# Hybrid decoder layer on one core: dilated tiles in groups of two, the narrow pattern's mask by a product and its sums on two engines, guards in groups of six

## The chip, the core and the metric

The kernel runs on one core of a Trainium2 chip. The metric is the device time of one execution in microseconds, as a median of several runs. Engines are named as in the profile: PE (TensorE, products), PEld (its weight loads), DVE (VectorE), ACT (ScalarE), POOL (GpSimd), SP (SyncE, which here issues nearly all transfers). The granted clock of PE is given as a share of its full rate.

## What is computed

One decoder layer over 2048 positions of width 1024. Eight heads of a dilated attention (three patterns of window and stride, with a linear bias per head, merged by their softmax denominators) and eight heads of a causal latent attention, each gated by SiLU, go through one output projection and a layer norm with the residual:

```python
DILATED_PATTERNS = ((128, 1), (512, 4), (2048, 16))

def _dilated_mixture(q, k, v):
    slopes = _alibi_slopes(q.shape[2])
    parts = [_dilated_pattern(q, k, v, slopes, w, d) for (w, d) in DILATED_PATTERNS]
    m_all = jnp.max(jnp.stack([pm for (_, pm, _) in parts], axis=0), axis=0)
    num = 0.0
    den = 0.0
    for acc, pm, pl in parts:
        wgt = jnp.exp(pm - m_all)
        num = num + acc * wgt[..., None]
        den = den + pl * wgt
    return num / den[..., None]
```

`_dilated_pattern` scores each query against the keys of its residue class in the window (`q.k / 8` minus slope times distance, masked by causality and window) and returns numerator, row maximum and denominator. All is float32.

## The kernel before

The program has five stages in a row, all unrolled: projections with keys and latent vectors (to 441 us), the gates with the guards (441 to 679), the dilated attention (679 to about 935), the latent attention (to about 1345), and the output projection with the layer norm.

*Order.* Every PE instruction goes through `Order` (`pe`), which pins them one behind the other as written. `pe.plan(work, span)` holds a list of side jobs, and `pe.tick()` after each main product lets one go whenever its share of `span` has passed. In the attention stages ACT is pinned the same way (`act`), and SP (`sp`). `later(units, f)` puts a job off by so many tiles; `go_on(w)`, called behind each tile's scores, counts them down and runs what is due. Loads of the next pair (`LT`), the rotated copies of its keys (`LTO`), and the steps of the division all go through it.

*Gates and guards.* 32 main tiles of 24 products (`m_tile`, a bank `mm` of six) make the SiLU gates. Between them run the guards: for each pair of heads 96 small rough score tiles in bfloat16 (32 for each pattern: keys contiguous, every 4th, every 16th), of which only the row maxima are wanted. `block(g)` (L752) does two guards: two products into one bank of the tag `nm` (two banks), then two reductions with the bias on DVE (L758). A pair's 48 blocks are followed by the load for the next pair, three empty items, `last` (transposes and scatters the maxima through DRAM), `GPAUSE` = 5 empty items; `write`, the fetch of the merged maxima, is set into the next pair's blocks at place `GW`. All items are spread over 623 main products.

*Dilated attention.* Four pairs of heads. A pair is a stream of 20 score tiles (`attend`, L962): four units of three tiles for the two wide patterns (two of stride 4, one of stride 16), then four units of two tiles for the narrow one. A tile's scores (`scores`, L967) are, for each of the two heads, a bfloat16 product `X` and an fp32r product `Y` (`KY`, `QY`), added in one PSUM bank of the tag `s` (four banks), and an exponential on ACT into `e` or `more` (seven buffers). Where `late(which)` holds (L965), `strike` (L983) zeroes what the mask forbids with selects on POOL (L990): two for stride 1 and 4, one for stride 16; otherwise a product of `identb` with the mask `msk` goes ahead of the scores. Before, that is so only for the narrow tiles of the last pair. `r_` then multiplies the values (`pv`, `o`). At a unit's end `finish` sums the exponentials into `acc`: on DVE, but in the last pair's narrow units on POOL (L1063 to L1068). One tile behind a narrow unit comes `epilogue(c)` (L1076): gate load, products of `ones` with `acc` (`l`), a copy `ls` on ACT (one buffer), its transfer `u<-ls` from ACT's queue, a reciprocal, and by way of DRAM (`sums`, `r`) the division of `g` and its store to `mixd`.

*Order in the dilated stage.* `chain(stream, g)` (L893) takes `g` tiles' scores, then the values of all held tiles but `LAG`. With `G2` = 1 and `LAG` = 1 the order is s2 r0 s3 r1: values run two tiles behind their scores. From the 13th tile of the last pair on, the guards of the latent attention (`mx<-k,ql`) are planned in between.

Of the kernel before, what the change touches and what calls it, by code (L numbers as in the profile page):

```python
# [9 lines left out]
F32 = mybir.dt.float32  # L10
# [8 lines left out]
P = 128  # L19
# [12 lines left out]
UQE = 20  # L32
SCB = 3
GFIRST = 4
GPAUSE = 5
LEAD = 42
K1T = (1.0, 6, 6.0)
WOT = (16, 18.5, 21, 26, 28, 30)
# [9 lines left out]
NL = 2**LEVELS - 1  # L48
EX = 3 + NL
UADD = 2  # L50
LAG = 1
XSB = 2
WARM = 12
GB = 2
GW = 9
RB = 2
HB = 2
SPL2 = 1
# [4 lines left out]
LTO = {(1, 0): (5, 6, 7, 8), (1, 1): (8.3, 9, 10, 11), (2, 0): (13, 14, 15, 16), (2, 1): (20.2, 21, 22, 23)}  # L63
KT3 = (1.0, 4.0, 14.0, 16.0, 18.0, 17.0, 7.0)
T2 = 0.4
G2 = 1
WSD = 0b0000
WSV = lambda g: WSD >> g & 1
MSV = lambda g: False
EPD = 1  # L70
EPL = 1
WP = 0
WL = 2
OB = 2
EB = 5
# [134 lines left out]
def body(ctx, tc, a, out):  # L210
# [104 lines left out]
    with ExitStack() as p1:  # L315
# [391 lines left out]
        with ExitStack() as p1g:  # L707
# [13 lines left out]
            def guard(p):  # L721
# [28 lines left out]
                            todo.append((n3(q, r), n3(k, r), P, e - 4, m[:, 2, h * 16 + r :]))  # L750

                def block(g):  # L752
                    o = ps.tile([P, 512], F32, tag="nm", name="mx", bufs=2)
                    for i, (q, k, n, e, dst) in enumerate(todo[g : g + 2]):
                        pe.matmul(o[:, i * 256 : i * 256 + n], q, k, start=True, stop=True)
                    for i, (q, k, n, e, dst) in enumerate(todo[g : g + 2]):
                        oi = o[:, i * 256 : i * 256 + n]
                        nc.vector.tensor_tensor_reduce(  # L758
                            out=oi, in0=oi, in1=bias[:, e, 256 - n : 256], scale=1.0,
                            scalar=-3.0e38, op0=ALU.add, op1=ALU.max, accum_out=dst[:, 0:1])  # L760
# [26 lines left out]
                    nc.vector.tensor_tensor(out=nm, in0=u[:, 0, :], in1=u[:, 2, :], op=ALU.min)  # L787
                    dma(nc.sync, out=dqe[2 * p : 2 * p + 2, EX - 1].rearrange("h (s j) -> h s j", j=P), in_=nm)

                return load, [(lambda g=g: block(g)) for g in range(0, 96, 2)], (last, write)  # L790

            extras = []
            for i, (dst, n) in enumerate(((dke, EX), (dqe[:, 0 : EX - 1], EX - 1))):
# [17 lines left out]
            for n, (i, c) in enumerate(seq):  # L811
                if n % 4 == 0 and n < 28:
                    w[n // 4 + 1] = load_w(gates[n // 4 + 1])
                if n == 0:
                    work = [guard(p) for p in range(PAIRS)]
                    work[0][0]()
                    dma(nc.sync, out=perm, in_=a["perm"])
                if n == 12:
                    for dst, src, w_ in ((msk[:, 0:512], a["mst"][:, 0:512], 512), (msk[:, 512:640], a["mst"][:, 512:640], 128),
                                         (mxb[:, 384:512], a["mxm"], 128)):  # L820
                        t = gp.tile([P, CH], F32, tag="v", name="mst", bufs=3)
                        dma(nc.sync, out=t[:, 0:w_], in_=src)
                        nc.gpsimd.tensor_copy(dst, t[:, 0:w_])
                if n == GFIRST:
                    items = []
                    for p, (_, blocks, (last, write)) in enumerate(work):
                        items += blocks + ([work[p + 1][0]] if p + 1 < PAIRS else []) + [pause] * 3 + [last]
                        items += [pause] * GPAUSE
                        if p:
                            items.insert(len(items) - len(blocks) - GPAUSE - 4 + GW, hold)  # L830
                        hold = write
                    items.append(hold)
                    pe.plan(items, (30 - GFIRST) * 24 - 1)
                if XT <= n < XT + len(extras):
                    extra(*extras[n - XT])
                o = m_tile(w[i], c)
                if n == 30:
                    gl = big([P, 2, CH], F32, "gl")
                g = gp.tile([P, CH], F32, tag="v", name="g", bufs=3) if n < 30 else gl[:, n - 30, :]
                (act if n == 31 else nc.scalar).activation(g, o, AF.Silu)  # L840
                dma(nc.sync, out=gat[i * P : (i + 1) * P, c * CH : (c + 1) * CH], in_=g)
                for k in {25: ("k0", "k1", "x0"), 27: ("q0", "x1", "q1"), 29: ("vb", "vc")}.get(n, ()):
                    loads[k]()
                if n >= 28:
                    x, h = ((1, 0), (1, 1), (2, 0), (2, 1))[n - 28]
                    for i in range(4):
                        loads["order"](h, x, i, nc.scalar.copy if i % 2 else nc.gpsimd.tensor_copy)
# [6 lines left out]
    with ExitStack() as p24:  # L854
# [107 lines left out]
        def attend(p, d):  # L962
            acc, osum = [], []

            late = lambda which: p < PAIRS - 1 or which > 0  # L965

            def scores(h, e, which, blocks, first):  # L967
                n = sum(w for _, _, w in blocks)
                s = spsum()
                if not late(which):  # L970
                    pe.matmul(s[:, 0:n], identb, msk[:, 0:n], start=True, stop=False)

                x = 0 if which == 2 and h and first else which
                for y, kq in enumerate("XY"):
                    kt_, qt = (d["X", h][:, 0], d["X", h][:, 1]) if kq == "X" else (d["KY", h, x if y else 0], d["QY", h])
                    off = 0
                    for i, (kf, qf, w) in enumerate(blocks):
                        pe.matmul(s[:, off : off + w], kf[y if x else 0](kt_), qf(qt), start=bool(late(which) and kq == "X" and i == 0),
                                  stop=(kq == "Y" and i == len(blocks) - 1))
                        off += w  # L980
                act.activation(e[:, h, 0:n], s[:, 0:n], AF.Exp, scale=0.125)

            def strike(e, which, n):  # L983

# [11 lines left out]
            def unit(specs, finish, more=None):  # L996
# [3 lines left out]
                def s_(i, w):  # L1000
                    which, blocks = specs[i][:2]
                    e = exps(True)
                    for h in range(2):
                        scores(h, e, which, blocks, first)
                        pe.tick(w * T2)
                    if late(which):
                        strike(e, which, sum(w_ for _, _, w_ in blocks))
                    es.append([e[:, h] for h in range(2)])
# [42 lines left out]
            for c in range(4):  # L1051
# [7 lines left out]
                def finish(o, es, c=c):  # L1059
                    for h in range(2):  # L1060
                        dst = acc[h][:, c * CH : (c + 1) * CH].rearrange("p (r b i) -> p b r i", r=16, b=4)
                        x1, x2 = (e[h].rearrange("p (b r i) -> p b r i", b=4, r=16) for e in es)
                        eng = nc.gpsimd if h < WP or (h < WL and p == PAIRS - 1) else nc.vector  # L1063
                        eng.tensor_add(dst, dst, x1)
                        eng.tensor_add(dst[:, 1:4], dst[:, 1:4], x2[:, 0:3])  # L1065
                        if c:
                            x2 = over[0][h].rearrange("p (b r i) -> p b r i", b=4, r=16)
                            eng.tensor_add(dst[:, 0], dst[:, 0], x2[:, 3])  # L1068
# [6 lines left out]

            def epilogue(c):  # L1076
                cols = slice(c * CH, (c + 1) * CH)
                g = ep.tile([P, 512], F32, tag="g", name="g", bufs=3)
                dma(sp, out=g, in_=gat[p * P : (p + 1) * P, cols])
                nc.vector.tensor_mul(nat(g), strip(osum[c]), nat(g))  # L1080
                divide(acc, cols, g, nat, p * NC + c,
# [94 lines left out]
        def attend3(i):  # L1176
# [13 lines left out]
            gate = []  # L1190

            def load_g():
                gate.append(ep.tile([P, 512], F32, tag="g", name="g3", bufs=3))
                dma(sp, out=gate[0], in_=gat[512 + p * P : 512 + (p + 1) * P, Q * CH : (Q + 1) * CH])

            def s_(two, ws):
# [314 lines left out]
```

## Time and profile before

| | us |
|---|---|
| runs | 1564.69 (median), 1565.36, 1556.76 |
| the profiled execution, as a run | 1558.75 |
| its span on the core | 1557.0 |
| gates and guards, 441 to 661 | 220.0 |
| dilated attention, first three pairs and the last one's wide patterns, 679.2 to 885.6 | 206.4 |

The span is counted from the first to the last instruction. In rows of a timeline `x4` counts instructions run together in the row, the first number is the start and the second the duration in microseconds; products overlap in the array, so the pace is read from one start to the next. In brackets stands how long the engine was idle ahead of the row, and what ended it.

### The profile page before, as it was taken

Reading aid. Unit: us, or ns where it says so; the run is one execution under the profiler, and the core shown is the slowest. Engines: PE = TensorE matmul, PEld = TensorE weight load, DVE = VectorE, ACT = ScalarE, POOL = GpSimd, SP = SyncE. Lnnn points to the kernel's source line nnn. Section 1 sums busy time; section 2 is a strip of 40 time slices with the busy share of each in tenths; the row PEclk is TensorE's granted clock in tenths of the full one; section 3 lists DMA queues with packets and bytes.
Section 4 is the critical chain, followed back from the end, with each engine's and each line's share of the span. In section 5 each row is a group of like instructions: output and inputs, shape, how many; then the busy total and the mean of one; then the engine's idle time right before and its main releaser. Section 6 shows DMA issues by size and latency. Waiting matters only on the chain.

```text
span 1557.0 us, 22893 instructions
## 1 busy us (share of the span) xinstructions
PE 1475.6 (95%) x8087; PEld 1039.4 (67%) x8088; DVE 948.3 (61%) x2123; ACT 510.9 (33%) x958; POOL 604.5 (39%) x504
## 2 busy tenths in 40 slices
PE   9999999999889999998887899899999999999997
PEld 6789987877766666676655654454555555478887
DVE  3121124455556767728878879677767757666575
ACT  5330033423321111056644523333333334532222
POOL 6300020234430001047868644334434435954443
PEclk9999999999999999999998899999999999999999
DMA  7551179777663421566677765623635613334442
GB/s 257 177 153 49 43 206 306 236 265 260 213 207 98 136 84 37 125 172 166 155 200 177 216 148 152 155 74 109 160 87 132 164 51 119 129 109 163 162 153 91
DMA packets 146167, 237.33 MB, mean 152 GB/s; under 512 B 28930, under 2 KB 69154, under 8 KB 141602
## 3 DMA queue, kind: packets, MB, share of 16 engines
q1 hardware_dynamic: 140996, 235.08, 51.3%
q8 instruction: 64, 1.05, 0.3%
q10 hardware_dynamic: 5056, 0.79, 0.3%
q14 instruction: 51, 0.42, 0.1%
HBM read 152.68 MB, written 82.94 MB: 151 GB/s over the span
## 4 chain that ended last, share of the span: by engine, by line
PE 40%; DVE 5%; DMA 5%; issue 2%; POOL 2%; ACT 1%; SPq 1%; ACTq 0%; POOLq 0%; DVEq 0%
PE s L168 25%; PE o L168 10%; PE mx L168 4%; DMA u<-ls 2%; DVE m L199 2%; PE l L168 1%; POOL e L990 1%; DVE g L199 1%; SPq L199 1%; DMA ql<-bqh 1%; DMA ql<-bql 1%; ACT e L199 1%; DVE acc L1065 0%; DMA sums<-u 0%; DVE mx L199 0%
## 5 line engine op out<-in xcount | busy, mean ns | idle before, releaser
L199 ACT ACTIVATE e<-s 128x512 f32<-128x512 f32 (+3 forms) x434 | 205.2, 546 | 246.2 <-PE s L168 121.9
L168 PE MATMUL mm<-xh,wh 128*128 128x512 f32 x544 | 225.5, 415 | 0.0
L168 PE MATMUL mm<-xh,wl 128*128 128x512 f32 x544 | 223.4, 411 | 0.2 <-POOL wl L435 0.2
L168 PE MATMUL mm<-xl,wh 128*128 128x512 f32 x544 | 223.2, 410 | 0.0
L199 POOL TENSOR_TENSOR ac<-ac,e 128x512 f32<-128x512 f32 (+3 forms) x128 | 158.0, 1235 | 161.1 <-ACT e L199 156.0
L168 PE MATMUL s<-ql,k 128*128 128x512 f32 (+3 forms) x640 | 183.5, 384 | 1.2 <-ACT e L199 1.1
L758 DVE CUSTOM_DVE_ANT_0 mx<-mx,bias 128x256 f32<-128x256 f32 (+1 forms) x384 | 140.0, 380 | 69.6 <-PE mx L168 49.0
L199 DVE TENSOR_REDUCE m<-mx 128x1 f32<-128x512 f32 x192 | 129.1, 688 | 68.0 <-PE mx L168 64.9
L168 PE MATMUL s<-wo,mh 128*128 128x512 f32 (+1 forms) x544 | 159.9, 377 | 0.0
L168 PEld LDWEIGHTS s<-ql,k 128*128 128x128 f32 x640 | 108.0, 190 | 61.9 <-ACT e L199 44.4
L168 PE MATMUL mx<-k,ql 128*128 128x512 f32 (+2 forms) x320 | 122.5, 405 | 16.3 <-DVE m L199 8.2
L168 PE MATMUL o<-e,vl 128*64 128x512 f32 (+3 forms) x640 | 137.8, 553 | 0.0
L348 POOL TENSOR_TENSOR wl<-ws,wh 128x1024 fp32r<-128x1024 f32 x16 | 38.3, 2396 | 246.4 <-ACT wh L347 227.5
L199 DVE TENSOR_TENSOR ac<-ac,e 128x512 f32<-128x512 f32 (+3 forms) x128 | 117.6, 919 | 7.1 <-ACT e L199 0.5
L168 PEld LDWEIGHTS mm<-xh,wh 128*128 128x128 f32 x544 | 104.1, 191 | 20.9 <-issue 0.8
L168 PEld LDWEIGHTS mm<-xh,wl 128*128 128x128 f32 x544 | 104.1, 191 | 20.1 <-POOL wl L435 0.5
L168 PEld LDWEIGHTS mm<-xl,wh 128*128 128x128 f32 x544 | 103.9, 191 | 20.1
L990 POOL TENSOR_SCALAR_AFFINE_SELECT e<-e 128x512 f32<-128x512 f32 (+2 forms) x90 | 100.9, 1151 | 39.1 <-issue 19.2
L168 PEld LDWEIGHTS s<-wo,mh 128*128 128x128 f32 x544 | 100.2, 188 | 19.4 <-issue 0.4
L168 PE MATMUL mx<-kh,qz 128*128 128x256 bf16 (+1 forms) x384 | 103.7, 357 | 4.8 <-DVE m L758 3.1
L168 PE MATMUL s<-wo,ml 128*128 128x512 f32 (+1 forms) x272 | 102.4, 377 | 0.0
L199 DVE CUSTOM_DVE_ANT_0 mx<-mx,mxb 128x128 f32<-128x128 f32 (+3 forms) x128 | 63.1, 497 | 52.0 <-PE mx L168 43.0
(212 smaller groups left out, 2603.0 us busy)
## 6 DMA issues: line engine op xcount, KB each, us to landing
ws<-wi SPq DMA_DIRECT2D x16, 512.0 KB
X<-dx SPq DMA_DIRECT2D x16, 512.0 KB
g<-gat SPq DMA_DIRECT2D x32, 256.0 KB
r<-sums SPq DMA_DIRECT2D x64, 128.0 KB
mixd<-g SPq DMA_DIRECT2D x32, 256.0 KB
k<-bkh SPq DMA_DIRECT2D x16, 512.0 KB
ql<-bqh SPq DMA_DIRECT2D x32, 256.0 KB
mf<-mixd SPq DMA_DIRECT2D x8, 1024.0 KB
```

The lines of the kernel that those rows point to most:

```text
L168: self._pin(self.tc.nc.tensor.matmul(out, lhsT, rhs, start=start, stop=stop))
L199: ins = getattr(self.engine, name)(*args, **kwargs)
L348: nc.gpsimd.tensor_sub(l[:, ks], t[:, ks], f32(h[:, ks]))
L758: nc.vector.tensor_tensor_reduce(out=oi, in0=oi, in1=bias[:, e, 256 - n : 256], scale=1.0, scalar=-3.0e38, op0=ALU.add, op1=ALU.max, accum ...
L990: nc.gpsimd.affine_select(out=v, in_=v, compare_op=ALU.is_ge, fill=0.0, base=0, pattern=[[0, v.shape[1]]] + [[sign * x, y] for x, y in pat ...
```

## The change

Scores are taken two tiles at a time and values follow for all tiles that were held (`G2` = 2, `LAG` = 0: s2 s3 r0 r1). Within a tile the products run X X Y Y over the two heads. All narrow tiles get their mask from the product with `identb`. In pairs 0 to 2 the narrow sums of head 0 run on POOL, those of head 1 on DVE. A guard block has six guards in three banks, one `nm` and two `mm`; the empty items are cut to fit the longer spacing. The gate tile `g` has four buffers.

```diff
-GPAUSE = 5
+GPAUSE = 2
+GBANKS = 3
-LAG = 1
+LAG = 0
-GW = 9
+GW = 3
-G2 = 1
+G2 = 2
-WP = 0
+WP = 1
 def block(g):
-    o = ps.tile([P, 512], F32, tag="nm", name="mx", bufs=2)
-    for i, (q, k, n, e, dst) in enumerate(todo[g : g + 2]):
-        pe.matmul(o[:, i * 256 : i * 256 + n], q, k, start=True, stop=True)
-    for i, (q, k, n, e, dst) in enumerate(todo[g : g + 2]):
-        oi = o[:, i * 256 : i * 256 + n]
+    todo_ = todo[g : g + 2 * GBANKS]
+    os = [ps.tile([P, 512], F32, tag="nm", name="mx", bufs=2) if i < 1 else mm() for i in range(GBANKS)]
+    for i, (q, k, n, e, dst) in enumerate(todo_):
+        pe.matmul(os[i // 2][:, i % 2 * 256 : i % 2 * 256 + n], q, k, start=True, stop=True)
+    for i, (q, k, n, e, dst) in enumerate(todo_):
+        oi = os[i // 2][:, i % 2 * 256 : i % 2 * 256 + n]
...
-    return load, [(lambda g=g: block(g)) for g in range(0, 96, 2)], (last, write)
+    return load, [(lambda g=g: block(g)) for g in range(0, 96, 2 * GBANKS)], (last, write)
...
-    items += blocks + ([work[p + 1][0]] if p + 1 < PAIRS else []) + [pause] * 3 + [last]
+    items += blocks + ([work[p + 1][0]] if p + 1 < PAIRS else []) + [pause] * 1 + [last]
...
-late = lambda which: p < PAIRS - 1 or which > 0
+late = lambda which: which > 0
-def scores(h, e, which, blocks, first):
+def scores(e, which, blocks, first, tick):
     n = sum(w for _, _, w in blocks)
-    s = spsum()
-    if not late(which):
-        pe.matmul(s[:, 0:n], identb, msk[:, 0:n], start=True, stop=False)
+    ss = [spsum() for h in range(2)]
+    for y in range(2):
+        for h in range(2):
+            s = ss[h]
+            if not y and not late(which):
+                pe.matmul(s[:, 0:n], identb, msk[:, 0:n], start=True, stop=False)
...
+            if y:
+                act.activation(e[:, h, 0:n], s[:, 0:n], AF.Exp, scale=0.125)
+        tick()
...
-    for h in range(2):
-        scores(h, e, which, blocks, first)
-        pe.tick(w * T2)
+    scores(e, which, blocks, first, lambda: pe.tick(w * T2))
...
-    eng = nc.gpsimd if h < WP or (h < WL and p == PAIRS - 1) else nc.vector
+    eng = nc.gpsimd if h < (WL if p == PAIRS - 1 else WP) else nc.vector
...
-g = ep.tile([P, 512], F32, tag="g", name="g", bufs=3)
+g = ep.tile([P, 512], F32, tag="g", name="g", bufs=4)
```

## Rows read from the trace of the kernel before

**Rows 1.** The page's first line: span and number of instructions.

```profile
span 1557.0 us, 22893 instructions
```

**Rows 2.** Windows: length, busy us of PE, PEld, DVE, ACT, POOL, clock, DMA.

```profile
441.00:661.00 220.00, 215.39 (x988) 143.22 (x989) 158.25 (x770) 27.12 (x44) 20.21 (x13) 1.00 0.37 107
679.20:732.80 53.60, 47.03 (x393) 33.82 (x392) 33.32 (x55) 32.30 (x54) 37.57 (x39) 0.90 0.61 154
732.80:791.10 58.30, 49.71 (x430) 34.69 (x428) 49.66 (x66) 32.72 (x53) 47.94 (x40) 0.94 0.73 177
791.10:851.20 60.10, 50.79 (x431) 35.12 (x430) 50.64 (x70) 34.07 (x56) 46.67 (x40) 0.91 0.68 176
851.20:885.60 34.40, 30.21 (x271) 22.03 (x269) 27.78 (x45) 18.30 (x33) 20.05 (x22) 0.90 0.75 205
```

**Rows 3.** PE's waits, 679.2 to 885.6 us: total, times, longest.

```profile
PE o L168 <- POOL e L990: 9.6, 6, 3.2
PE l L168 <- DVE acc L1068: 6.4, 5, 1.7
PE l L168 <- DVE acc L1065: 6.4, 6, 2.6
PE o L168 <- POOL more L990: 2.4, 3, 1.3
```

**Rows 4.** Timeline of PE, tiles of the first pair without waits.

```profile
694.19 1.08 PE L168 MATMUL o<-e,vb 128*64 128x256 f32 x8
695.21 0.41 PE L168 MATMUL s<-X 128*128 128x256 bf16 x2
...
696.28 0.87 PE L168 MATMUL o<-e,vb 128*64 128x256 f32 x8
697.08 0.35 PE L168 MATMUL s<-X 128*128 128x256 bf16 x2
```

**Rows 5.** Timeline in the second pair: the longest wait for a mask.

```profile
764.65 1.08 PE L168 MATMUL o<-e,va 128*64 128x256 f32 x8 [2.57 <-POOL e L990]
765.67 0.60 PE L168 MATMUL s<-X 128*128 128x256 bf16 x2
```

**Rows 6.** Timeline of SP and ACT at the second pair's end.

```profile
771.55 1.44 SPq L199 DMA_DIRECT2D X<-dx  x2
...
779.65 0.53 ACTq L199 DMA_DIRECT2D u<-ls  x1
...
793.55 0.37 ACT L199 COPY ls<-l 128x256 f32<-128x256 f32 x1 [9.54 <-DMA u<-ls]
```

**Rows 7.** Lines L1064 and L990: duration in ns, least, median, greatest.

```profile
L1064 DVE TENSOR_TENSOR acc<-acc,e x18: 677/1482/1516, 714.1 to 857.7; 128x512 f32<-128x512 f32 x18
...
L1064 POOL TENSOR_TENSOR acc<-acc,e x6: 1260/1269/1568, 887.4 to 920.0; 128x512 f32<-128x512 f32 x6
...
L990 POOL TENSOR_SCALAR_AFFINE_SELECT e<-e x90: 439/1090/4939, 685.0 to 885.4; 128x512 f32<-128x512 f32 x64, 128x256 f32<-128x256 f32 x14, 128x1024 f32<-128x1024 f32 x12
```

**Rows 8.** Timeline of PE, last pair: the mask's product, then the scores.

```profile
885.60 0.39 PE L168 MATMUL s<-msk,identb 128*128 128x512 bf16 x1
885.83 0.38 PE L168 MATMUL s<-X 128*128 128x256 bf16 x2
```

**Rows 9.** Timeline of PE among the guards: main products around three blocks.

```profile
482.58 0.40 PE L168 MATMUL mm<-xh,wl 128*128 128x512 f32 x1
...
483.40 0.40 PE L168 MATMUL mm<-xh,wh 128*128 128x512 f32 x1
483.63 0.40 PE L168 MATMUL mm<-xh,wl 128*128 128x512 f32 x1
...
484.57 0.39 PE L168 MATMUL mm<-xh,wh 128*128 128x512 f32 x1
...
485.55 0.39 PE L168 MATMUL mm<-xl,wh 128*128 128x512 f32 x1
```

**Rows 10.** PE's waits among the guards, 441 to 661 us.

```profile
PE mx L168 <- DVE m L758: 3.1, 2, 2.9
```

More of the change, by code (lines that the diff above doesn't have):

```diff
@@ L963, in attend @@
             acc, osum = [], []
-            late = lambda which: p < PAIRS - 1 or which > 0
-            def scores(h, e, which, blocks, first):
+            late = lambda which: which > 0
+            def scores(e, which, blocks, first, tick):
                 n = sum(w for _, _, w in blocks)
-                s = spsum()
-                if not late(which):
-                    pe.matmul(s[:, 0:n], identb, msk[:, 0:n], start=True, stop=False)
[L973 to L981, printed above, removed]
+                ss = [spsum() for h in range(2)]
[4 more added lines that the diff above has]
+                            pe.matmul(s[:, 0:n], identb, msk[:, 0:n], start=True, stop=False)
+                        x = 0 if which == 2 and h and first else which
+                        kt_, qt = (d["KY", h, x], d["QY", h]) if y else (d["X", h][:, 0], d["X", h][:, 1])
+                        off = 0
+                        for i, (kf, qf, w) in enumerate(blocks):
+                            pe.matmul(s[:, off : off + w], kf[y if x else 0](kt_), qf(qt),
+                                      start=bool(late(which) and not y and i == 0), stop=bool(y and i == len(blocks) - 1))
+                            off += w
+                        if y:
+                            act.activation(e[:, h, 0:n], s[:, 0:n], AF.Exp, scale=0.125)
+                    tick()
             def strike(e, which, n):
@@ L1192, in load_g @@
             def load_g():
-                gate.append(ep.tile([P, 512], F32, tag="g", name="g3", bufs=3))
+                gate.append(ep.tile([P, 512], F32, tag="g", name="g3", bufs=4))
                 dma(sp, out=gate[0], in_=gat[512 + p * P : 512 + (p + 1) * P, Q * CH : (Q + 1) * CH])
```

## Prediction

> **What bounds the kernel now.** I read the stages' windows first, then what TensorE (PE) waited for in the dilated stage, then single tiles on PE's timeline. The profiled execution has a span of 1557.0 us [rows 1] and took 1558.75 us as a run. The change touches two stages, and the windows show them to be of different kinds [rows 2]. In the stage of the gates (441 to 661 us) PE is busy 215.4 of 220.0 us at full clock: it is simply full. In the dilated stage the four windows (three whole pairs of 53.6, 58.3 and 60.1 us, and the wide patterns of the last pair, 34.4 us) are 206.4 us together, PE's granted clock is 0.90 to 0.94, and neither VectorE (DVE) nor GpSimd (POOL) has much room: in the second pair 49.7 and 47.9 of 58.3 us.
>
> PE's waits in that stretch [rows 3] are of two kinds: values that wait for masks made by POOL (9.6 + 2.4 = 12.0 us in nine waits), and row sums `l` that wait for DVE's sums (6.4 + 6.4 = 12.8 us in eleven). The clock costs more: full-rate work lost is 0.10 x 53.6 + 0.06 x 58.3 + 0.09 x 60.1 + 0.10 x 34.4 = 17.7 us [rows 2]. It falls behind the long waits: after a wait of 2.57 us for a mask, the next score products take 0.60 instead of 0.41 us [rows 4, 5]. So some 42 us of this stage are waiting and its price in clock; that is what the change can win. A third thing waits and isn't touched: the copy `ls` of the row sums on ScalarE (ACT) stood 9.54 us until the transfer `u<-ls` of the block before had left, which was issued at 779.65, eight microseconds behind the loads of the next pair (`X<-dx` at 771.55) [rows 6].
>
> **The change, part by part.** *Mask by a product.* In pairs 0 to 2 the eight narrow tiles lose two selects each on POOL (48 in all, median 1.09 us [rows 7]: 52 us of POOL) and get a product with `identb` for each head. The last pair has these products already: 885.60 to 885.83, 0.23 us for 512 columns [rows 8]. 21 tiles of 512 and 3 of 384 columns, two heads: 21 x 0.46 + 3 x 0.345 = **+10.7 us** on PE. Bounds: 0 if it all falls into waits that stay, 10.7 if PE is full.
>
> *Two tiles at a time.* Order before: s2 r0 s3 r1; after: s2 s3 r0 r1. Between values and the next scores PE loses time: a values tile of 2048 streamed columns takes 1.02 us (694.19 to 695.21), one of 1536 takes 0.80 (696.28 to 697.08) [rows 4]. So 512 columns cost 0.22, and of the 1.02 some 0.14 to 0.18 is the turn; I take 0.18. Half the turns go: 36 of the 72 tiles before the last pair's narrow ones, **-6.5 us**. Bounds: 0 if turns merely move, -13 if the turn from scores to values costs as much. Inside a tile the products are now X X Y Y instead of X Y X Y; I take nothing for it, since the columns are the same, and the first exponential is ready only some 0.3 us later.
>
> *Mask waits.* Between a tile's scores and its values lie now, for both tiles of a group, two more score tiles and two values, about 4.8 us; before it was 3.1 (one score tile, a value, a score tile, at 1.07 and 1.02) [rows 4]. A tile's two selects at 1.09 and its exponentials fit 4.8 more often than 3.1, and the narrow tiles' masks are gone altogether. Of 12.0 us I let 2 stay: **-10 us** (bounds -12 and -4).
>
> *Sums shared.* In pairs 0 to 2 head 0's three adds of a narrow unit go from DVE to POOL. On DVE the 512-wide add took 0.68 us at the least and 1.48 at the median; on POOL, in the last pair, 1.27 [rows 7]. DVE's part of a narrow unit halves; POOL loses four selects (4.4 us) and gains about 2.5 us (1.27 scaled from 512 to 1024 elements, an estimate). `l` is issued where it was: a narrow unit ends with an odd tile, so its sums are still issued behind the same score tile, and the epilogue one tile later. Its transfers on SyncE's queue (gate load, `sums`, `r`, `mixd`) therefore keep their place behind the next pair's loads, and so do the rotated copies of the keys on ACT and POOL. I let half of the 12.8 us go: **-6.4 us** (bounds -12.8, and a loss, below).
>
> *Clock.* Two thirds of the listed waits go by these sums (16.4 of 24.8); I give half of the 17.7 us back: **-9 us** (bounds 0 and -17.7).
>
> *Guards six at a time.* 192 blocks of two become 64 of six. Two main products and a block between them take 0.82 us with 384 strided columns, 0.94 with 512, and 0.98 with 256 columns of the widest stride; a main product takes 0.23 [rows 9]. That leaves 0.36 and 0.48 for the first two: in the ratio of the columns, 3 to 4, with nothing left for the block itself. So fewer blocks save little: **-1 us** (0 to -4). On the other side, six guards give DVE 6 x 0.41 = 2.5 us of work in one go (158.3 us busy over 384 guards [rows 2]); PE's period for six is 220 / 64 = 3.4, so DVE keeps up and one group of banks in reserve suffices. The blocks now take two of the six `mm` banks each time, which only the main tiles had. The maxima's transpose and the next pair's loads of `kh` and `qz` come 22 rather than 13 ticks behind the last block: later, but no PE wait hangs on them.
>
> *Rest.* A fourth buffer `g` lets a gate load start earlier; it is hidden by the 256 KB's place in the queue and gives 0. Seven buffers of exponentials stay: a wide unit's first tile is now freed behind the sixth score tile instead of the fifth, while the eighth needs it. That slack shrinks from three tiles to two, about 4 us, against four sums of DVE at 0.7 to 1.5; I take 0.
>
> Sum: 10.7 - 6.5 - 10 - 6.4 - 9 - 1 = **-22.2 us**, 1558.75 - 22.2 = 1536.6, say **1537**. It stands against the profiled run, which is 5.9 below the median of the three runs (1564.69) and 2 above the fastest.
>
> **The rivals.** *A. The sums on POOL become the wait* (the other side). POOL works in order: head 0's sums can stand behind two selects of the next wide tiles (2.2 us) and take 2.5 themselves, while PE gives them one score tile with its products, 1.5 us. That is 3.2 us in each of the 12 narrow units, 38 against 12.8 now: 10.7 - 6.5 - 6 + 25 - 1 = +22, **1581 us**, with no clock won back. It decides once `l` waits over 2.6 us a unit. For it: DVE's adds at 1.48 against 0.68 show that the two engines hinder each other [rows 7]. Against it: the selects that filled POOL in the narrow part are gone, and a sum there needs no mask first. The Trainium skill's page "SBUF — State Buffer", section "SBUF: two separate sides", says that DVE instructions with two SBUF inputs and POOL's take one port pair in turn, whole instructions at a time; by that rule sharing the sums wins nothing (0.68 + 1.27 instead of twice 0.68), and the term of -6.4 would be 0. The spread of the adds agrees with it in kind.
>
> *B. The transfers pin the pair.* The next pair's loads still stand ahead of `u<-ls`; from `X<-dx` to the copy that waited it was 22 us [rows 6]. If that sets when the second half of a pair ends, PE only comes sooner to the same wait, and part of the masks and sums won is given back there: 10.7 - 6.5 - 6 - 2 - 3 = -6.8, **1552 us**. For it: SyncE, DVE and ACT all queue behind that transfer. Against: no single wait of PE for `l` was over 2.6 us [rows 3].
>
> *C. Everything goes:* 10.7 - 13 - 12 - 12.8 - 17.7 - 4 = -48.8, **1510 us**. Against it: the transfer above.
>
> *D. The guards' banks:* a main tile or a block waits for a bank once in most tiles, 4 or 5 times by 2.5 us: +12, **1549 us**. Against it: PE waits for DVE only twice there now, 3.1 us in all [rows 10].
>
> **How the numbers follow.** Chances: forecast 0.45, A 0.12, B 0.25, C 0.13, D 0.05. A measurement of this kernel tells about 1% from no change: under 1549.0 us is faster, over 1580.3 slower (of 1564.69). Faster takes 0.42 of the forecast, C, and a little of B and D: 0.60; slower most of A and an unforeseen tenth of the rest: 0.10; within 1%: 0.30. The range leaves out most of C below and half of A above: 1515 to 1569; the forecast's own is 1526 to 1549.
>
> **What would show it.** Right: in the dilated windows a clock of 0.95 or more, pairs of about 51 us, PE waits for POOL under 3 us, `l` waits under 7 us, the `identb` products at 0.23 each, the guards' window 219 to 221 us. Wrong: `l` waiting for POOL's sums (A); ACT's `ls` still waiting 20 us and pairs over 55 us (B); waits of `mm` or `mx` for DVE or ACT in the guards' window (D). Were mask waits to stay in the wide patterns, the longer distance was not what counted.

## The result, and the profile after

The changed kernel takes 1544.6 us (median of 4 runs, 1543.7 to 1551.3) against 1563.4 of the kernel before (4 runs): a ratio of 0.989, 95% interval 0.986 to 0.992, 18.8 us less. In a second set, beside other kernels, it took 1545.4 against 1564.5, 0.988 (0.985 to 0.990). The forecast was 1537; the time lies inside its own range of 1526 to 1549, 7.6 us above the sum. The profiled execution after took 1545.07 us, 13.7 less than the one of before.

The span of the changed kernel, to set beside [rows 1]:

```profile
span 1543.3 us, 22895 instructions
```

Its windows, cut where the stages now begin (the columns are those of [rows 2]): the guards, the three whole pairs, the wide patterns of the last pair.

```profile
443.80:655.60 211.80, 208.28 (x982) 152.29 (x982) 138.27 (x764) 27.16 (x44) 20.70 (x13) 0.99 0.37 110
676.30:725.70 49.40, 45.55 (x410) 35.03 (x409) 26.82 (x46) 31.63 (x54) 32.38 (x35) 0.93 0.64 162
725.70:778.50 52.80, 48.21 (x446) 35.57 (x445) 38.52 (x56) 31.67 (x53) 36.30 (x35) 0.97 0.73 185
778.50:835.90 57.40, 50.42 (x445) 37.06 (x446) 40.16 (x59) 33.18 (x56) 37.55 (x35) 0.91 0.74 192
835.90:869.60 33.70, 29.07 (x270) 22.75 (x271) 23.77 (x40) 17.76 (x33) 22.00 (x21) 0.90 0.81 230
```

The pairs became 4.2, 5.5 and 2.7 us shorter and the wide patterns of the last pair 0.7, 13.1 together where 21.2 were forecast. The guards' stretch, 220.0 us before, became 8.2 us shorter where 1 us was forecast (below).

What PE waited for in the dilated stretch after, 676.3 to 869.6 us (us in all, times, longest):

```profile
PE s L169 <- ACT e L200: 7.2, 5, 2.7
PE o L169 <- DVE osum L1051: 4.3, 2, 2.2
PE s L169 <- DMA QY<-dq: 3.8, 2, 2.1
PE s L169 <- ACT more L200: 2.2, 2, 2.0
PE o L169 <- POOL e L998: 1.4, 3, 1.0
```

Against [rows 3], the two kinds of wait that the forecast went after are gone: masks from 12.0 to 1.4 us, row sums `l` from 12.8 to nothing that is listed. In their place PE waits for exponentials (7.2 and 2.2, against 2.3 before), for a copy on DVE (4.3) and for a transfer (3.8).

One profiled execution can be read this finely only if executions of one code agree, so this table sets the same stretches of all the profiled kernels side by side: the guards' stretch from the first product of the fifth gate tile to that of the last, pairs 0 to 2 from the first score product with `KY` to that of the last pair, and from there to the second step of the latent attention. All in us, from the starts of these products.

| kernel | guards | pairs 0 to 2 | last pair and first latent step |
|---|---|---|---|
| before | 233.0 | 172.0 | 128.2 |
| guards_six_alone | 223.7 | 172.1 | 132.4 |
| product_alone | 230.7 | 161.9 | 131.6 |
| select_to_scratch | 230.8 | 164.8 | 134.2 |
| product_and_guards | 224.1 | 159.1 | 136.3 |
| changed | 226.0 | 159.6 | 128.0 |
| changed_again (same code) | 225.3 | 163.7 | 128.2 |
| guards_by_two | 232.1 | 164.3 | 130.1 |
| one_at_a_time | 226.0 | 164.9 | 128.8 |
| one_ls_two | 224.4 | 162.0 | 132.1 |
| sums_on_dve | 223.1 | 164.5 | 129.1 |
| ls_two | 225.0 | 163.3 | 132.9 |
| select_sums_dve | 224.8 | 172.0 | 127.5 |
| select_mask | 223.8 | 178.7 | 124.3 |

The guards' column falls into two groups, 230.7 to 233.0 with blocks of two and 223.1 to 226.0 with blocks of six. Pairs 0 to 2 of one code scatter by some 5 us (159.6, 163.7 and 164.3 for the changed code).

### The profile page after: what moved, and what is told of

It reads as the page before. It is cut to its first block, busy times and chain, and to the rows that moved or that the text cites. A ratio compares the mean times of both kernels' runs of the same rounds, so it can differ in the third digit from the quotient of the medians.

```text
span 1543.3 us, 22895 instructions
## 1 busy us (share of the span) xinstructions
PE 1469.5 (95%) x8136; PEld 1056.3 (68%) x8136; DVE 895.1 (58%) x2090; ACT 506.7 (33%) x958; POOL 579.7 (38%) x489
## 4 chain that ended last, share of the span: by engine, by line
PE 36%; DVE 7%; DMA 4%; issue 2%; POOL 1%; ACT 1%; SPq 0%; ACTq 0%; POOLq 0%; DVEq 0%
PE s L169 23%; PE o L169 9%; PE mx L169 4%; DVE m L200 2%; DMA u<-ls 2%; PE l L169 1%; DMA ql<-bqh 1%; POOL wo L1344 1%; DVE g L960 1%; DVE acc L1046 1%; DMA X<-dx 1%; DVE acc L1047 1%; DVE mx L200 1%; DVE g L200 0%; SPq L200 0%
## 5 line engine op out<-in xcount | busy, mean ns | idle before, releaser
L169 PE MATMUL mm<-xh,wh 128*128 128x512 f32 x544 | 218.2, 401 | 0.1
L169 PE MATMUL mm<-xh,wl 128*128 128x512 f32 x544 | 217.3, 399 | 0.1
L169 PE MATMUL mm<-xl,wh 128*128 128x512 f32 x544 | 216.8, 398 | 0.0
L169 PEld LDWEIGHTS s<-wo,mh 128*128 128x128 f32 x544 | 100.1, 188 | 19.3 <-issue 0.4
L761 DVE CUSTOM_DVE_ANT_0 mm<-mm,bias 128x256 f32<-128x256 f32 (+1 forms) x256 | 93.7, 390 | 6.5 <-PE mm L169 3.1
L169 PEld LDWEIGHTS mx<-k,ql 128*128 128x128 f32 x320 | 61.1, 193 | 46.9 <-DVE m L200 27.8
L761 DVE CUSTOM_DVE_ANT_0 mx<-mx,bias 128x256 f32<-128x256 f32 (+1 forms) x128 | 51.2, 400 | 71.4 <-PE mx L169 59.7
## 6 DMA issues: line engine op xcount, KB each, us to landing
r<-sums SPq DMA_DIRECT2D x64, 128.0 KB
```

The lines of the kernel that those rows point to most:

```text
L169: self._pin(self.tc.nc.tensor.matmul(out, lhsT, rhs, start=start, stop=stop))
L761: nc.vector.tensor_tensor_reduce(out=oi, in0=oi, in1=bias[:, e, 256 - n : 256], scale=1.0, scalar=-3.0e38, op0=ALU.add, op1=ALU.max, accum ...
```

## The experiments

All ratios are against the kernel before, on the same chip in the same minutes. The changed kernel itself is at 0.989 and 0.988.

**Theories.** By the forecast, each part of the change pays for itself: product and later values against masks, pairs against turns, shared sums against the row sums' waits. The rival, which took shape from the profile after and from the first of the runs below: two parts carry all of it, the guards and the mask's product, and the product does so by what it takes off POOL.

### The guards, undone and alone

```diff
-GPAUSE = 2
-GBANKS = 3
+GPAUSE = 5
+GBANKS = 1
...
-GW = 3
+GW = 9
...
-items += blocks + ([work[p + 1][0]] if p + 1 < PAIRS else []) + [pause] * 1 + [last]
+items += blocks + ([work[p + 1][0]] if p + 1 < PAIRS else []) + [pause] * 3 + [last]
```

> The changed kernel with its guards as before (blocks of two guard products, longer pauses); the dilated attention is as changed. The changed kernel stands at 0.989 of the kernel before (1544.6 against 1563.4 us). The forecast's own term (guards worth 1 us): 1545.6, 0.990, and the guards' section, from the first to the last gate product group, within 1 us of the changed kernel's. The rival, read from the two traces after the result (the section became 7 us shorter, a block of six costs less than three of two because each block has a fixed cost of its own): 1551 to 1552, 0.993 to 0.994, all of the difference before the first dilated tile.

Measured: 1550.6, 0.992 (0.989 to 0.994). The stretch is back at 232.1 us. The other way round, the same edit made in the kernel before and nothing else:

> The kernel before with nothing but the guards changed: six guard products a block, with the shorter pauses. The forecast's term (1 us): 1562, 0.999 of the kernel before. What the run with the guards undone showed (4 us between medians, 9 us between the section's two ends in the profiles): 1559 to 1555, 0.997 to 0.995, the stretch from gate group 4 to gate group 31 6 to 9 us shorter than its 233.0 us of before, and the rest as it was.

Measured: 1555.9, 0.994 (0.992 to 0.996), 10.6 us by the medians; the stretch went from 233.0 to 223.7. So the guards are worth 4 to 11 us, not 1. A block of six in the changed kernel, on PE's timeline:

```profile
485.15 0.40 PE L169 MATMUL mm<-xh,wl 128*128 128x512 f32 x1
485.39 0.64 PE L169 MATMUL mx<-kh,qz 128*128 128x256 bf16 x2
485.85 1.14 PE L169 MATMUL mm<-kh,qz 128*128 128x128 bf16 x4
486.63 0.59 PE L169 MATMUL mm<-xl,wh 128*128 128x512 f32 x1
487.06 0.39 PE L169 MATMUL mm<-xh,wh 128*128 128x512 f32 x1
```

From 485.15 to 487.06 are 1.91 us, less two main products of 0.23 leaves 1.45 for the six. As three blocks of two the same guards cost 0.48 + 0.52 + 0.52 = 1.52 [rows 9]. Over all undisturbed blocks, worked out in the same way, six together save 0.05 to 0.11 us against three blocks of two, which is an estimate of about 0.07 x 64 = 4.5 us. All 192 blocks of before cost 83.6 us beyond the main products; the 64 of the kernel with the guards alone cost 74.1. The other 5 us are single late blocks, PE's waits among them; how they divide was not followed further.

### The mask's product, undone and alone

```diff
-late = lambda which: which > 0
+late = lambda which: p < PAIRS - 1 or which > 0
```

> The changed kernel with the narrow tiles of pairs 0 to 2 masked by POOL's selects again, without the product of the mask with the identity; the rest as changed. By the forecast's terms the product costs PE 10.7 us and takes 10 us of mask waits away: without it 1544, 0.988, PE's waits for POOL's masks back from 1.4 to 8 to 12 us and PE's busy time down by 10. A first rival (two tiles at a time and the later values hide the selects, so the product is pure cost): 1535, 0.982, waits for POOL under 4 us. A second (the selects now stand behind POOL's share of the sums): 1552 or more, 0.994, waits for POOL over 18 us.

Measured: 1562.9, 1.000 (0.998 to 1.002): without the product nothing is left of the whole gain. Its profiled run took 1549.5 us, the shortest of its 12, so the profile understates the loss; even so PE's waits in pairs 0 to 2 are these:

```profile
PE o L169 <- POOL e L998: 20.8, 13, 3.7
PE o L169 <- POOL more L998: 6.3, 4, 2.7
```

and that stretch took 178.7 us, at a granted clock of 0.87 with POOL busy 160.7 of it:

```profile
670.50:849.10 178.60, 145.64 (x1249) 107.64 (x1248) 114.19 (x164) 97.31 (x165) 160.65 (x147) 0.87 0.66 172
```

27 us in pairs 0 to 2 against 12.0 before: by the second rival the masks now stand behind POOL's share of the sums. If so, the waits must go when that share is taken back too. The next run does this, with the selects kept (`late` as above and `WP = 0`):

> The changed kernel with POOL's selects for the narrow masks and with all sums of pairs 0 to 2 on DVE: the two-tile order and the guards alone are left of the change. With the selects alone taken back it stood at 1.000 with PE waiting 31 us for POOL's masks. If these waits come from the selects standing behind POOL's share of the sums: back to 10 to 14 us of waits for POOL, 1548 to 1552, 0.991 to 0.993. If two tiles at a time by themselves want their masks sooner than POOL gives them: still over 22 us of waits for POOL, 1558 or more, 0.997 or more.

Measured: 1552.8, 0.991 (0.989 to 0.993), the first answer by the time; the waits for masks, 3.6 us, fell below both. Pairs 0 to 2, and what PE waited for there:

```profile
675.00:847.00 172.00, 145.22 (x1251) 106.55 (x1249) 131.79 (x189) 96.93 (x163) 128.57 (x118) 0.90 0.68 172
```

```profile
PE l L169 <- DVE acc L1071: 13.1, 11, 5.2
PE s L169 <- ACT e L200: 2.8, 3, 1.5
...
PE o L169 <- POOL e L998: 2.2, 4, 0.8
PE o L169 <- POOL more L998: 1.4, 3, 0.7
PE l L169 <- DVE acc L1074: 1.0, 3, 0.4
```

This is the two-tile order with the selects of before. Mask waits fall to 3.6 us, as the forecast's longer distance said, but the row sums wait 14.1 instead of 10.1 (6.4 for L1068 as in [rows 3], and the line below, both in pairs 0 to 2), the exponentials cost 5.5 instead of 2.3, and the stretch is 172.0 us, as before. The wait moved from the masks to other places, to the row sums most of all.

```profile
PE l L168 <- DVE acc L1065: 3.7, 5, 2.5
```

Now the product alone, in the kernel before (the diff above read the other way round):

> The kernel before with nothing but the narrow masks changed: a product of the mask with the identity for pairs 0 to 2 too, in place of POOL's selects; one tile at a time, sums on DVE. The forecast's terms (10.7 us of products, 10 us of waits): 1564, 1.000, PE's waits for POOL from 12.0 to under 3 us and the dilated stretch within 2 us of its 250.4. The rival (taking one tile at a time in the changed kernel cost nothing, so the product, and what rests on it, carries the gain): 1550 to 1553, 0.991 to 0.993, the dilated stretch near 240 us.

Measured: 1555.4, 0.993 (0.991 to 0.996), 11 us by the medians. Pairs 0 to 2 went from 172.0 to 161.9. Their window, and PE's waits for masks and row sums there (no other row is above 3.0 us):

```profile
678.00:839.90 161.90, 150.18 (x1299) 106.94 (x1297) 105.27 (x190) 99.67 (x163) 67.89 (x72) 0.94 0.71 178
```

```profile
PE o L168 <- POOL more L990: 2.1, 1, 2.1
...
PE o L168 <- POOL e L990: 0.7, 1, 0.7
...
PE l L168 <- DVE acc L1065: 0.3, 1, 0.3
```

The masks' waits are gone (12.0 to 2.8), and so are those of the row sums for DVE (10.1 to 0.3), though nothing was done to DVE: it runs 190 instructions as before, but is busy 105.3 us instead of 133.6. The window of before, for comparison:

```profile
679.30:851.30 172.00, 147.53 (x1250) 103.62 (x1250) 133.62 (x190) 98.99 (x163) 132.17 (x118) 0.92 0.67 170
```

The narrow sum's 512-wide add shows why (least, median and greatest ns), in the kernel before and with the product alone:

```profile
L1064 DVE TENSOR_TENSOR acc<-acc,e x16: 677/1482/1516, 714.1 to 842.5; 128x512 f32<-128x512 f32 x16
...
L1064 DVE TENSOR_TENSOR acc<-acc,more x6: 1491/1504/1516, 720.1 to 849.0; 128x512 f32<-128x512 f32 x6
```

```profile
L1064 DVE TENSOR_TENSOR acc<-acc,e x16: 672/685/693, 710.9 to 827.0; 128x512 f32<-128x512 f32 x16
L1064 DVE TENSOR_TENSOR acc<-acc,more x6: 684/690/693, 716.0 to 831.3; 128x512 f32<-128x512 f32 x6
```

All but one of the 22 adds of before (1.15 us) took either some 0.68 or some 1.48 us; with the product alone, where no POOL instruction was running as one of them began, all took the first. Set beside POOL's instructions in the trace of before, each of the 17 adds above 1 us from 679.2 to 885.6 us began while a select was running and ended 0.47 us after that select.

### POOL's work without its wait

The next kernel has the product and keeps the selects, which write to a tile that nobody reads (shown are the new tile and the calls; `strike` takes the tile as a further argument, and `late` is as in the kernel with the product). It does more work than the kernel with the product alone, none less.

```diff
+spare3 = ep.tile([P, 512], F32, name="spare3")
...
 if late(which):
     strike(e, which, sum(w_ for _, _, w_ in blocks))
+elif p < PAIRS - 1:
+    strike(e, which, sum(w_ for _, _, w_ in blocks), spare3)
```

> The kernel before with the product of the mask for the narrow tiles of pairs 0 to 2, as in the run with the product alone (1555.4 us, 0.993), and POOL nevertheless runs the selects of these tiles as before, but writes them to a spare tile that nobody reads: POOL's work is there, the wait for the masks is not. If the product won because nobody waits for POOL's masks any more: still 0.993, DVE's busy time over pairs 0 to 2 near 105 us. If it won because POOL's selects slowed DVE's sums next to them (1170 against 685 ns for the 128x512 add of the narrow sums), and the row sums waited for those: DVE back to 125 us or more, PE's waits of the row sums for DVE back from 0.3 to 8 us or more while its waits for POOL stay under 4 us, and 1560 to 1566, 0.998 to 1.002.

Measured: 1559.6, 0.997 (0.995 to 0.998), between the two answers. Pairs 0 to 2, the waits there, and the same add:

```profile
677.40:842.20 164.80, 151.93 (x1299) 106.26 (x1297) 133.57 (x191) 98.95 (x163) 128.69 (x116) 0.95 0.68 173
```

```profile
PE l L168 <- DVE acc L1072: 5.3, 6, 1.7
PE o L168 <- POOL e L995: 2.8, 4, 1.0
...
PE o L168 <- POOL more L995: 1.2, 1, 1.2
```

```profile
L1071 DVE TENSOR_TENSOR acc<-acc,e x16: 678/683/1493, 711.5 to 832.8; 128x512 f32<-128x512 f32 x16
L1071 DVE TENSOR_TENSOR acc<-acc,more x6: 679/1492/1492, 715.3 to 840.5; 128x512 f32<-128x512 f32 x6
```

DVE's busy time is back at 133.6, half of the row sums' waits is back (5.3 of 10.1), and 6 of the 11 us that the product saved are lost by the medians. In the stretch of pairs 0 to 2 itself less is lost, 2.9 of 10.1 us. PE's waits for masks are 4.0 us here and 2.8 with the product alone, so at most 1.2 us of the loss is POOL being late for the wide patterns. So a part of the product's gain, between three tenths and a half, is DVE's freedom from POOL, and the rest is that nobody waits for these masks any more; the runs do not divide it more finely.

### The two-tile order and the shared sums

```diff
-LAG = 0
+LAG = 1
...
-G2 = 2
+G2 = 1
```

> The changed kernel with the dilated tiles taken one at a time again, values one tile behind their scores; masks by products, shared sums and guards of six stay. The forecast's term (each turn from values to scores costs PE some 0.17 us, and half of the turns go): 6.5 us, so 1551, 0.993. The rival (turns are hidden or are replaced by the waits for exponentials that only the pairs of tiles show, 7.2 us of PE's waits): 1544 or less, 0.988 or less, with the waits of scores for the exponentials down from 7.2 to under 2 us.

Measured: 1541.6, 0.986 (0.983 to 0.989): no slower than the whole change, if anything faster. The window of pairs 0 to 2 in this kernel, in the changed one, and in the changed one again:

```profile
672.30:837.20 164.90, 148.36 (x1299) 105.96 (x1297) 100.69 (x160) 97.32 (x163) 103.54 (x104) 0.94 0.69 174
```

```profile
676.50:836.00 159.50, 144.08 (x1298) 107.57 (x1297) 105.50 (x160) 96.28 (x163) 106.23 (x104) 0.94 0.71 181
```

```profile
674.60:838.30 163.70, 144.44 (x1300) 109.55 (x1298) 105.07 (x160) 96.20 (x163) 109.89 (x104) 0.93 0.69 175
```

In pairs PE is busy 4 us less at the same clock, so turns do cost and half of them do go. The two kernels with the second buffer (below) show it too: less the work lost to the clock, as the prediction works it out, PE is busy 138 to 139 us one at a time (two profiles) and 133 to 135 in pairs (three). What is left of the window is waiting: 16.5 us one at a time, 15.4 and 19.3 in pairs. In the second profile of the changed kernel most of it is this, 12.5 us against 7.1 (4.2 and 2.9) one at a time:

```profile
PE s L169 <- ACT e L200: 8.1, 5, 4.6
PE s L169 <- DMA X<-dx: 4.4, 2, 2.4
```

The shared sums alone taken back (`WP = 0`):

> The changed kernel with all narrow sums of pairs 0 to 2 on DVE again. The forecast's term (sharing halves DVE's work ahead of the row sums): 6.4 us, so 1551, 0.993, with PE's waits of the row sums for DVE's sums back at 6 us or more. First rival (the pairs' ends are set by the transfer that the reciprocal waits for, which sharing does not move): 1544 to 1545, 0.989, pairs 0 to 2 within 1 us each. Second rival (POOL and DVE working on the same side slow each other, so that sharing itself cost): 1540 or less, 0.985, with DVE's narrow sums nearer to their shortest times.

Measured: 1548.3, 0.990 (0.988 to 0.993), by the first rival if by any: 2 to 4 us above the changed kernel's two sets, inside the interval. `l` does not wait for DVE's sums in that run either. But the second rival's sign came: DVE's sums are near their shortest times again. DVE is busy 105.9 us here with 190 instructions, and 105.5 in the changed kernel with 160, while POOL is busy 65.7 and 106.2. Sharing took 30 instructions off DVE and no time. The window, and the same add with all sums on DVE and with sums shared:

```profile
672.00:836.40 164.40, 146.72 (x1298) 109.76 (x1297) 105.94 (x190) 96.31 (x163) 65.72 (x72) 0.91 0.69 176
```

```profile
L1070 DVE TENSOR_TENSOR acc<-acc,e x18: 672/678/693, 704.4 to 844.3; 128x512 f32<-128x512 f32 x18
```

```profile
L1070 DVE TENSOR_TENSOR acc<-acc,e x9: 673/1378/1754, 709.9 to 842.8; 128x512 f32<-128x512 f32 x9
```

Single adds show how. In the changed kernel POOL's add began first, and DVE's, 0.44 us behind it, ended 0.55 us after it. In the kernel with the selects kept DVE's add began 0.05 us ahead and took 0.69, and POOL's took 1.76 instead of 1.27 [rows 7]. The one that begins second pays:

```profile
713.79 1.29 POOL L1070 TENSOR_TENSOR acc<-acc,more 128x512 f32<-128x512 f32 x1 [0.87 <-ACT more L200]
714.23 1.40 DVE L1070 TENSOR_TENSOR acc<-acc,more 128x512 f32<-128x512 f32 x1 [0.89 <-ACT more L200]
```

```profile
704.96 0.69 DVE L1070 TENSOR_TENSOR acc<-acc,e 128x512 f32<-128x512 f32 x1 [2.69 <-POOL e L998]
705.01 1.76 POOL L1070 TENSOR_TENSOR acc<-acc,e 128x512 f32<-128x512 f32 x1
```

Both parts left out at once, the two-tile order and the shared sums, that is the product and the guards put into the kernel before:

> The kernel before with two parts of the change: the products of the narrow mask and the guards of six; tiles still one at a time, each head's scores together, sums of pairs 0 to 2 on DVE. Alone they stood at 0.993 and 0.994. If they add up: 0.987, 1545 us, no slower than the whole change, whose other parts are then worth nothing. If the two-tile order and the shared sums carry something that the profiles' scatter hides: 0.990 or more, and the whole change below it by 3 us or more.

> The changed kernel once more, beside the others on one chip: 0.986 to 0.990. Its dilated stretch (233.5 us from the first dilated tile to the first latent scores in its first profile, 239.9 in the run with only the guards taken back, which has the same code there) says how far one execution's stretch can be read: within 1 us of 233.5 if the difference came from the guards' edit, near 237 to 240 if it is scatter between executions.

Measured on one chip: 1547.0, 0.989 (0.987 to 0.992), and 1545.4, 0.988 (0.985 to 0.990). The 1.6 us between them lie within the intervals. The one line of `late` and the guards' blocks give what the whole change gives, within what can be measured here. The second profile of the changed kernel has 237.5 us from the first dilated tile to the first latent scores where the first had 233.5, the same code.

### The transfer behind the loads

```diff
-LSB = 1
+LSB = 2
...
-t = ep.tile([8, P], F32R, tag="mt", name="mt3", bufs=2)
+t = ep.tile([P, 256], F32R, tag="ls", name="mt3", bufs=LSB)[0:8, 0:P]
```

> The changed kernel with a second buffer for the row sums that ACT copies for the small transfer to the reciprocal (the [8,128] tile of the latent guards shares these buffers to make room). ACT waits 16.7 us for the first buffer, and the exponentials stand behind it on ACT. If that wait is where the two-tile order loses its gain: PE's waits for exponentials from 7.2 (and 2.2 for the other name of their buffers) to under 3 us, 1538 to 1540, 0.984 to 0.985. If the transfer itself pins the pair's end: the wait moves on to the reciprocal on DVE and the pairs stay within 1 us, 1544, 0.989.

Measured: 1545.0, 0.986 (0.983 to 0.989). ACT's waits in pairs 0 to 2 with the second buffer (the first row; none is for `ls`):

```profile
ACT e L200 <- PE s L169: 27.8, 18, 4.2
```

In the changed kernel the copy `ls` still stood behind the transfer, from 676.3 to 869.6 us as follows, 8.7 of it in pairs 0 to 2. Now it waits no more:

```profile
ACT ls L200 <- DMA u<-ls: 16.7, 3, 8.3
```

Yet pairs 0 to 2 took 163.3 us, inside the 159.6 to 164.3 of the changed code: the wait was there and set nothing that can be seen. The same buffer with tiles one at a time:

> The changed kernel with tiles one at a time (0.986 in its own run) and two buffers for the copied row sums (0.986 with tiles two at a time). If ACT's wait for the row sums' transfer still holds the exponentials up in this order (4.2 us of PE's waits): 0.983, 1540 us. If it is covered: 0.986, as without the second buffer.

Measured: 1544.5, 0.987 (0.985 to 0.990): covered. No run here was clearly faster than the changed kernel.

## Why the prediction was right, and where it wasn't

The time fell in the forecast's own range, and mask waits and row sums went as it said. But its sum did not come about by its terms, and that it came so near is in good part luck.

**Mask waits, -10, with the product at +10.7.** The sizes held as far as they go: masks 12.0 to 1.4 us, and the product's 0.23 us stands in the changed kernel too (0.22 and 0.23 us on PE's timeline at 759.29 and 761.97). Either of the two edits takes most of these waits by itself: with the product alone 2.8 us are left, with two tiles at a time alone 3.6. The distance was misread on the way: by `chain` two values and two score tiles lay between a tile's scores and its values before, not one value and two score tiles, so by the forecast's own prices it grew from 4.2 to 5.2 us, not from 3.1 to 4.8. The step that failed is that the two were taken as the whole account of this edit, +0.7 net. The product is worth -11 by itself. For pairs 0 to 2 the profiles of before and of the product alone add up: what PE is not busy goes from 24.5 to 11.7 us (-12.8), its busy time from 147.5 to 150.2 (+2.7), together the 10.1 measured. The +2.7 can be made up, as an estimate, of +10.7 for the products, -3.9 for the row-sum products, which no longer stall one by one (11.8 to 7.9 us busy), and -4.1 for the clock (172.0 x 0.08 less 161.9 x 0.06).

**Sums shared, -6.4.** Sized rightly as a wait that would go, but given to the wrong edit. The row sums waited for DVE, whose adds took 1.48 us beside POOL's selects; the product removed these selects, and with them 9.8 of 10.1 us. With the selects back in a spare tile 5.3 us of these waits came back, so about half is shown to be DVE's slower adds. The other half went with the masks themselves, for which DVE's narrow sums stood 3.4 us before; how it came about was not followed further. Sharing had nothing left to win, and it would have won little on DVE in any case: DVE's busy time is the same with shared sums and without, 105.5 and 105.9 us. The sentence at the end of rival A bears on this: the Trainium skill's page "SBUF — State Buffer", section "SBUF: two separate sides", has DVE instructions with two SBUF inputs and POOL's take turns for whole instructions. The traces agree with it: long adds begin while a POOL instruction runs and end 0.47 to 0.55 us after it, and of two adds side by side the one that begins second is the long one. The rule put the term of -6.4 at 0, and no run shows it clear of the noise (2 to 4 us, inside the interval). The forecast weighed the rule only against the sums that POOL takes on, not for the selects that it loses.

**Rival A** did not come in the changed kernel. A relative of it is real: with the selects kept, POOL's sums cost 0.9% (1.000 against 0.991), some 14 us. But there it is the masks that stand behind POOL's sums (27.1 us of PE's waits), not `l` that waits for sums behind the masks, as A had it. What decides is whether the masks have left POOL first. The parts of this change are no list of separate terms.

**Two tiles at a time, -6.5.** The turns went as forecast, 4 us of PE's busy time in pairs 0 to 2. The step that failed was to take the exponentials' cover as unchanged: two tiles' scores now come in a row, take all four banks `s` with their two heads, and wait for the banks that ACT's exponentials free: 6.8 and 10.3 us in the two profiles after, against 2.3 before and 6.2 and 2.5 in the two kernels that take the changed kernel's tiles one at a time. In the last pair the two-tile kernels took 124 to 133 us to the second latent step (seven profiles, mean 128.6), those with one tile at a time 128 to 136 (seven, mean 131.9); that may be a gain of 3 us, but part of this scatter is the clock (last section), and no total shows it. It stays open.

**Clock, -9.** The loss in the four dilated windows after is 0.07 x 49.4 + 0.03 x 52.8 + 0.09 x 57.4 + 0.10 x 33.7 = 13.6 us against 17.7: -4, although the waits that the forecast listed are nearly all gone. New waits took the old ones' place (20.3 us listed after, 29.3 before), which may be why; no run separates it. The 0.95 named as a sign came in one pair of three. And no term stands for the stage behind: the first latent step took 54.1 and 54.4 us in the two profiles of the changed kernel, 49.9 in that of before (last section).

**Guards, -1.** The mis-sized term: 9.3 us in the profiles of the guards alone, 7.0 between the means of ten and four profiles. "Nothing left for the block itself" came from fitting two costs to two blocks by the ratio of their columns; a block has some 0.03 to 0.05 us of its own, and single blocks that met a late engine make up the rest. Rival D did not come: PE waits there after as follows, beside 3.1 us for DVE before [rows 10].

```profile
PE mm L169 <- ACT g L843: 2.8, 1, 2.8
PE mm L169 <- DMA qz<-aqn: 0.7, 1, 0.7
```

**Rival B** was half right in its signs (`ls` still waited 16.7 us, the third pair 57.4 us) and wrong in its conclusion, as the second buffer showed. **Rival C** (1510) did not come: exponentials, a copy and a transfer took the place of the waits that went.

Put by edits, the forecast had the product with the waits and the clock that hang on it at -14.7 (10.7 - 10 - 6.4 - 9), the turns at -6.5 and the guards at -1; measured were -11, nothing that a total shows, and -4 to -11. The sum was good because the guards gave back what the other two fell short of; nothing in the forecast said that they would.

## What to carry to other kernels

Before costing an engine's relief by the waits for that engine alone, look at the least and the median of its neighbour's durations: 0.68 against 1.48 us on DVE meant that work taken from POOL would pay a second time, on DVE, and that work moved from DVE to POOL would not. Where two edits aim at waits of one stretch, ask which would be left if only one were made. And where a stage of the same code comes out 4 us apart in two executions, a difference of that size between two profiles is not yet a reading; how a third and a fourth kernel come out there tells more.

## What the runs showed of the hardware

DVE's add of 128x512 with both inputs in SBUF is long or short by what POOL was doing as it began. In the fourteen profiles 114 of these adds in the narrow units began with no POOL instruction under way, and every one took 0.67 to 0.70 us. Another 118 began beside a select or an add of POOL and ended 0.47 to 0.55 us after it, which made them up to 1.75 us long. The other 20 were short although POOL was busy: with five, POOL's instruction ended within 10 ns; with 15, it was a long one (1.6 to 5.1 us) that ended 0.9 us or more after the add. POOL pays in the same way when it begins second: in the run with the selects kept, its add of the same size took 1.71 us in the mean, where the last pair had shown 1.27 before [rows 7].

The granted clock of one stage differs between kernels that run the same instructions there. The first step of the latent attention, which the guards do not touch, before and with the guards alone:

```profile
929.71:979.56 49.85, 46.58 (x234) 24.27 (x232) 43.99 (x78) 16.26 (x35) 20.98 (x15) 1.00 0.61 157
```

```profile
925.24:978.43 53.19, 49.52 (x234) 25.30 (x232) 44.23 (x78) 16.25 (x35) 20.69 (x15) 0.94 0.57 149
```

PE's share and the count of instructions are the same; 0.06 x 53.2 = 3.2 us is the difference. In the changed kernel's profile this step ran at 0.91 and took 54.1 us, and the gain seemed to shrink by 4 us there. It does not look like the chance of one execution: the second profile of the changed kernel has 54.4 us at 0.91, and all five profiles of two tiles at a time with the mask's product have 0.91. Six others have 0.94 (53.2 to 55.1 us), that of the selects kept 0.97, and only before and the selects to a spare tile 1.00 (49.9 and 50.2). So the step's clock seems to go with the kernel, that is with what ran ahead of the step; what sets it no run here shows.

The medians differ by 18.8 us and the two profiles by 13.7 because the profiled execution of before was 4.7 us below its median, and that of after 0.5 above. Where in the program those 4.7 us lie is not known. One stretch that the change leaves alone shows such scatter: the fifth gate tile began at 440.0 us in the profile of before, at 443.8 and 442.7 in those of the changed kernel, and between 439.7 and 444.2 in all fourteen.
